# An attention layer on one core: one split of the residual, norm weights folded into the matrices, another order of its stages

## The chip, the core and the metric

One core of one Trainium2 chip runs the whole program in one launch. The metric is the device time in microseconds of that launch; the median of several runs is compared. TensorE multiplies matrices into PSUM, VectorE, ScalarE and GpSimd work elementwise, and SyncE's queue issues nearly all DMAs.

## What is computed

A two-layer decoder trunk, 512 tokens of width 1024, float32. Layer 0 is a gated linear attention and a convolutional FFN. The change lies in layer 1, a sparse attention (NSA) of 16 query heads over 4 key/value heads, followed by another FFN. Cut to what matters:

```python
kv = (rmsnorm(x, g_kv) @ w_kv)          # 6 parts: raw k, raw v, k_sel, v_sel, k_win, v_win
k_cmp, v_cmp = compress_blocks(kv[0]), compress_blocks(kv[1])   # gelu(blocks @ w1) @ w2
k_sel, k_win = rope(kv[2]), rope(kv[4])
h = rmsnorm(x, norm_mix[1])
q, gates = split(h @ w_in); gates = sigmoid(gates)
o = gates[0] * softmax(q k_cmp) v_cmp + gates[1] * softmax(rope(q) k_sel) v_sel \
  + gates[2] * softmax(rope(q) k_win) v_win
x = x + o @ w_o
```

With 512 tokens the selection takes all blocks and the window all keys, so the selected and the window branch are causal attentions with their own keys and values. `rmsnorm(x, g)` is `x * r * g` with one factor `r` per token and one weight `g` per feature.

## The kernel before

Every large product is made of three float32r products: a weight and an activation are each split into a high part `h` (ScalarE copies to float32r) and a low part `l` (the rest, by a subtraction), and `mm3` (lines 207 to 211) adds h*h, l*h and h*l. `load_w` (142) loads a matrix of 128 x 1024 into one of three `w_raw` buffers by SyncE's queue, and writes `w_h` on ScalarE and `w_l` on VectorE, or on GpSimd with `pool=True`; two buffers each. `split_x` (160) makes the eight splits of the residual `xT` times a norm weight; `squares` and `rms` (187, 200) make the token factor: the sum of squares partly on GpSimd, `rc` by a power on GpSimd, then `pb` (four transposes on TensorE) and `rb` on ScalarE.

The layer is `nsa_att` (582). Ahead of the heads it makes, each with 24 TensorE products: the first two queries `Q` (`query`, 621), the gates (607), the four key tiles (`keys_in`, 648), the raw keys and values (`raw_in`, 724, with VectorE's `kb`), and `compress` (678): VectorE's `blk`, products `ph` in two halves of 16, Gelu on ScalarE into `G`, products `pk`. `values_in` (662) makes V in 96 products of 256 columns. `rope` (593) swaps halves through one buffer `sw` by four DMAs and multiplies on GpSimd (`rot`, `sw`), and VectorE adds; `queries` (629) makes `q_s` of it.

The loop over 16 heads (892) interleaves `scores(h+1)` with `values(h)`. `scores` (769) makes for each block of 128 tokens `sc` on TensorE, the maximum `nm` on VectorE, the exponential `p_t` and its sum `su` on ScalarE, and scales `p_t`, by the engine that a letter of SCALE_ENGINE names (P is GpSimd, D VectorE, A ScalarE; places (i, b) = 00, 01, 10, 11, 20, 21, 30, 31). `values` (824) transposes `p_t` into `tp`, splits it into `pt_h` and `pt_l`, and multiplies with V into `po`; every second head closes a tile `o` with its split `o_h`, `o_l` (863). Queries and parts of the output product `pw` (`wo_part`, 579) are placed behind heads by QUERY_HEAD and WO_HEAD with a lowered priority. A scheduler sets the final order of each engine's queue from program order and priorities; each queue then runs strictly in that order.

## Time and profile before

| | |
|---|---|
| median of 3 runs | 1355.27 us (1353.68 to 1357.93) |
| the profiled execution | 1355.55 us |
| its span | 1353.8 us |
| TensorE busy | 1321.1 us (98%) |
| VectorE, ScalarE, GpSimd busy | 909.4, 617.4, 171.5 us |

The rows further down come from one profiled execution; times count from the start of its span. The layer begins where the last product of layer 0's FFN ends, at about 627.6 us, its heads run from about 757 to 955, and the rest of the output product ends at about 980. An engine's idle time ahead of an instruction stands in square brackets with what ended it.

### The profile page before, as it was taken

What the parts mean: (1) busy time and instruction counts of PE and PEld (TensorE: products, weight loads), DVE (VectorE), ACT (ScalarE), POOL (GpSimd) and SP (SyncE); (2) the same over time, 40 slices, a digit from 0 to 9 for tenths busy, and PEclk for the clock granted to TensorE, in tenths of its full rate; (3) what the DMA queues carried; (4) which work ended last, traced back from release to release, by engine and by line L of the source; (5) the groups of instructions that cost most, each with busy time, mean ns of one, the idle gap of its engine ahead of it and who ended that gap; (6) DMA issues with size and microseconds to landing.
All of it is one profiled execution on the core that took longest, in us unless ns stands there. A gap on an engine that the chain in (4) does not pass through costs nothing. (4 is left out here: it accounts for less than half of the span.)

```text
span 1353.8 us, 17497 instructions
## 1 busy us (share of the span) xinstructions
PE 1321.1 (98%) x6592; PEld 1082.1 (80%) x6592; DVE 909.4 (67%) x1408; ACT 617.4 (46%) x1032; POOL 171.5 (13%) x238
## 2 busy tenths in 40 slices
PE   8999999999999999999989999999999999999998
PEld 4988987888888888887779777777788888888886
DVE  6877665477636763674875898988767735773671
ACT  4444434344413431443436677777644423441341
POOL 3000001200000000003322444442200000000000
...
GB/s 181 75 63 63 61 50 78 94 94 94 96 95 104 95 93 93 94 82 146 127 174 63 73 46 35 44 55 32 89 114 94 93 96 98 103 93 94 94 109 63
DMA packets 40261, 119.79 MB, mean 88 GB/s; under 512 B 5344, under 2 KB 6240, under 8 KB 40176
## 3 DMA queue, kind: packets, MB, share of 16 engines
...
q14 instruction: 33, 0.27, 0.1%
...
## 5 line engine op out<-in xcount | busy, mean ns | idle before, releaser
L148 ACT ACTIVATE w_h<-w_raw 128x1024 fp32r<-128x1024 f32 (+3 forms) x198 | 200.2, 1011 | 312.9 <-PE pd L211 129.9
L211 PE MATMUL pu<-x_l,w_h 128*128 128x512 f32 x704 | 274.1, 389 | 0.0
L209 PE MATMUL pu<-x_h,w_h 128*128 128x512 f32 x704 | 274.1, 389 | 0.0
L210 PE MATMUL pu<-x_h,w_l 128*128 128x512 f32 x704 | 273.9, 389 | 0.0
L150 DVE TENSOR_TENSOR w_l<-w_raw,w_h 128x1024 fp32r<-128x1024 f32 (+3 forms) x184 | 221.1, 1202 | 50.8 <-ACT w_h L148 48.8
L211 PEld LDWEIGHTS pu<-x_l,w_h 128*128 128x128 f32 x704 | 132.2, 188 | 27.5
L210 PEld LDWEIGHTS pu<-x_h,w_l 128*128 128x128 f32 x704 | 132.2, 188 | 27.4
L209 PEld LDWEIGHTS pu<-x_h,w_h 128*128 128x128 f32 x704 | 132.2, 188 | 27.2
L209 PE MATMUL pd<-m_h,w_h 128*128 128x512 f32 x304 | 120.2, 395 | 0.0
L211 PE MATMUL pd<-m_l,w_h 128*128 128x512 f32 x304 | 120.1, 395 | 0.0
L210 PE MATMUL pd<-m_h,w_l 128*128 128x512 f32 x304 | 120.0, 395 | 0.0
L258 DVE TENSOR_TENSOR u<-pu,rb 128x512 f32<-128x512 f32 x88 | 60.6, 689 | 83.1 <-PE pu L211 81.0
L236 DVE TENSOR_TENSOR xall<-xall,pd 128x512 f32<-128x512 f32 x40 | 27.5, 688 | 100.9 <-PE pd L211 100.9
L257 POOL MEMSET u<- 128x2 f32 x88 | 8.4, 100 | 604.3 <-DVE cv L263 604.3
L155 ACT ACTIVATE m_h<-cv 128x512 fp32r<-128x512 f32 x44 | 27.8, 631 | 115.6 <-DVE cv L266 115.6
L796 ACT ACTIVATE p_t<-sc,nm 128x128 f32<-128x128 f32 (+3 forms) x128 | 66.9, 528 | 11.9 <-DVE nm L789 7.5
L260 ACT ACTIVATE cv<-u,cols 128x512 f32<-128x512 f32 x88 | 71.1, 808 | 2.6 <-DVE u L258 1.8
L209 PEld LDWEIGHTS pd<-m_h,w_h 128*128 128x128 f32 x304 | 57.1, 188 | 14.1 <-ACT m_h L155 0.4
L211 PEld LDWEIGHTS pd<-m_l,w_h 128*128 128x128 f32 x304 | 57.1, 188 | 14.0 <-DVE m_l L157 0.2
L263 DVE SCALAR_TENSOR_TENSOR cv<-u,cols,cv 128x512 f32<-128x512 f32 x88 | 66.2, 752 | 3.0
L210 PEld LDWEIGHTS pd<-m_h,w_l 128*128 128x128 f32 x304 | 57.1, 188 | 13.7
L262 DVE SCALAR_TENSOR_TENSOR cv<-u,cols,cv 128x512 f32<-128x512 f32 x88 | 65.7, 747 | 2.0 <-ACT cv L260 1.9
...
## 6 DMA issues: line engine op xcount, KB each, us to landing
w_raw<-in_ffn_up_dram SPq DMA_DIRECT2D x88, 512.0 KB, 3.6
w_raw<-in_ffn_down_dram SPq DMA_DIRECT2D x32, 512.0 KB, 3.5
w_raw<-in_gla_v_dram SPq DMA_DIRECT2D x8, 512.0 KB, 3.6
w_raw<-in_gla_r_dram SPq DMA_DIRECT2D x8, 512.0 KB, 3.6
w_raw<-in_gla_o_dram SPq DMA_DIRECT2D x8, 512.0 KB, 3.6
w_raw<-in_nsa_q_dram SPq DMA_DIRECT2D x8, 512.0 KB, 3.6
w_raw<-in_kv_f_dram SPq DMA_DIRECT2D x8, 512.0 KB, 3.7
...
```

Of the source, the lines that this page charges most:

```text
L148: ACT.activation(h, raw, AF.Copy)
L150: (POOL if pool else DVE).tensor_tensor(l, raw, h, OP.subtract)
L155: ACT.activation(h, src, AF.Copy)
L209: PE.matmul(ps, wh, xh, start=first, stop=False)
L210: PE.matmul(ps, wl, xh, start=False, stop=False)
L211: PE.matmul(ps, wh, xl, start=False, stop=last)
L236: DVE.tensor_tensor(xT[d], xT[d], ps, OP.add)
L258: DVE.tensor_tensor(u[:, 2:], ps, rb[0], OP.mult)
L260: ACT.activation(c, u[:, 2:2 + S], AF.Identity, scale=col(w, 3 * jj + 2), bias=col(f"conv_b{layer}", jj))
L262: DVE.scalar_tensor_tensor(c, u[:, 1:1 + S], col(w, 3 * jj + 1), c, OP.mult, OP.add)
L263: DVE.scalar_tensor_tensor(c, u[:, 0:S], col(w, 3 * jj), c, OP.mult, OP.add)
L796: ACT.activation(pr[i, b], scv[:, bi], AF.Exp, bias=nm[:, i, b:b + 1], accum_out=su[:, i, b:b + 1])
```

## The change

The residual is split once, without a norm weight; the norm weights `kv` and `mix1` are multiplied into the rows of each raw matrix in its buffer, on GpSimd, ahead of its split (21 matrices). Ahead of the heads come the raw keys and values first, then two of the four key tiles, the first query, `compress` with `values_in` around it, the gates and the second query; `scores(0)` comes last. Six queries and the other two key tiles go between heads (FILL). Query weights' low halves move from GpSimd to VectorE. Per head, two more of the eight scalings of `p_t` go from VectorE to GpSimd, and `o_l` goes there too. `kx` gets another buffer group.

```diff
--- before.py
+++ after.py
@@ -27,8 +27,8 @@
 ATT_END = 1664
 INTERLEAVE = "ssvsvsvsvs"
 SCORE_GROUPS = ((0, 1), (3, 2))
-SCALE_ENGINE = "PDDDDDAP"
-QUERY_HEAD = (0, 2, 4, 6, 8)
+SCALE_ENGINE = "PDDPDPAP"
+FILL = {0: ("q", (0, 1)), 1: ("q", (1, 1)), 3: ("q",), 4: ("q",), 6: ("q",), 8: ("q",)}
 WO_HEAD = (9, 10, 10, 11, 11, 12, 12, 14)
 
 COLS = {}
@@ -48,7 +48,7 @@
                ("conv_w0", 132), ("conv_w1", 132), ("conv_b0", 44), ("conv_b1", 44)])
 
 
-TAGS = {"sq0": "y1", "x_h": "xs", "x_l": "xs", "kx": "pt_h", "gz": "pt_h", "lo": "sq", "o_t": "sq", "w2": "sq", "qn": "qo", "o_h": "qo", "o_l": "qo", "kb": "qo",
+TAGS = {"sq0": "y1", "x_h": "xs", "x_l": "xs", "kx": "qo", "gz": "pt_h", "lo": "sq", "o_t": "sq", "w2": "sq", "qn": "qo", "o_h": "qo", "o_l": "qo", "kb": "qo",
         "pz": "ps", "pvt": "tp", "pqk": "ps", "plv": "ps", "pc": "pn", "pb": "pn", "pgt": "pn", "pC": "pn", "pT": "pn",
         "ph": "pj", "pk2": "pj", "G": "sq", "gr": "rot", "blk": "p_t", "w1": "pt_l", "w1b": "pt_h", "w1c": "p_t"}
 TAGS.update({f"scan{n}": "scan" for n in (64, 128, 256)})
@@ -139,10 +139,14 @@
         at = COLS[name][0] + i
         return cols[:, at:at + n]
 
-    def load_w(src, shape, raw=None, pool=False):
+    def load_w(src, shape, raw=None, pool=False, gain=None):
+
         if raw is None:
             raw = T(shape, F32, "w_raw")
             nc.sync.dma_start(raw, src)
+        if gain is not None:
+            with tc.high_priority(offset=300):
+                POOL.tensor_tensor(raw, raw, col(*gain, shape[1])[:, :, None].to_broadcast(shape), OP.mult)
         with tc.high_priority(offset=300):
             h = T(shape, F32R, "w_h")
             ACT.activation(h, raw, AF.Copy)
@@ -210,19 +214,19 @@
         PE.matmul(ps, wl, xh, start=False, stop=False)
         PE.matmul(ps, wh, xl, start=False, stop=last)
 
-    def proj(src, xs, name, w=None, pool=False, m=128):
+    def proj(src, xs, name, w=None, pool=False, m=128, gain=None):
         n = len(xs)
-        h, l = w or load_w(src, [128, n, m], pool=pool)
+        h, l = w or load_w(src, [128, n, m], pool=pool, gain=gain and (gain, 0))
         ps = P(name)
         for k in range(n):
             mm3(ps[0:m], (h[:, k], l[:, k]), xs[k], k == 0, k == n - 1)
         return ps
 
-    def proj_tok(src, xs, name):
+    def proj_tok(src, xs, name, gain=None):
 
         pv = [P(name) for _ in range(2)]
         for kp in range(2):
-            h, l = load_w(src[kp], [128, 4, 256])
+            h, l = load_w(src[kp], [128, 4, 256], gain=gain and (gain, 4 * kp))
             for kk in range(4):
                 k = 4 * kp + kk
                 for i in range(4):
@@ -580,11 +584,10 @@
         add_x(d, proj(a["nsa_o"][d][:, k0:k0 + 4], os_[k0:k0 + 4], "pw", pool=k0 == 0))
 
     def nsa_att():
-        xq = [split_x("mix1")]
+        xs = [split(xT[k], "x") for k in range(KT)]
         acc = squares()
-        early = [proj(a["nsa_q"][0], xq[0], "tp")]
+        first = proj(a["kv_f"][0], xs, "sc", gain="kv")
         rb, r4 = rms(acc)
-        early.append(proj(a["nsa_q"][1], xq[0], "tp"))
         cosT = T([128, S], F32, "cosT")
         sinT = T([128, S], F32, "sinT")
         nc.sync.dma_start(cosT, a["rope"][0])
@@ -605,7 +608,7 @@
         gate = T([128, 4, 3, 16], F32, "gate")
 
         def gates():
-            pg = proj(a["nsa_g"], xq[0], "po", m=48)
+            pg = proj(a["nsa_g"], xs, "po", m=48, gain="mix1")
             gz = T([48, S], F32, "gz")
             DVE.tensor_tensor(gz, pg[0:48], rb[0:48], OP.mult)
             pgt = P("pgt")
@@ -619,7 +622,7 @@
         Q = []
 
         def query():
-            ps = early[len(Q)] if len(Q) < 2 else proj(a["nsa_q"][len(Q)], xq[0], "pl", pool=True)
+            ps = proj(a["nsa_q"][len(Q)], xs, "pl", gain="mix1")
             q = T([128, S], F32, "qn")
             DVE.scalar_tensor_tensor(q, ps, 0.125, rb, OP.mult, OP.mult)
             Q.append(q)
@@ -645,22 +648,21 @@
 
 
         K = [T([128, 2, S], F32R, f"K{g}") for g in range(4)]
-        def keys_in(br):
-            for ft in range(2):
-                ps = proj(a["kv_f"][4 + 2 * br + ft], xk[0], "sc")
-                k = T([128, S], F32, "kx")
-                DVE.tensor_tensor(k, ps, rb, OP.mult)
-                kr = rope(k)
-                for hh in range(2):
-                    hs = slice(hh * 64, hh * 64 + 64)
-                    kt = K[2 * ft + hh]
-                    ACT.activation(kt[0:64, br], kr[hs], AF.Copy)
-                    DVE.tensor_tensor(kt[64:128, br], kr[hs], kt[0:64, br], OP.subtract)
+        def keys_in(br, ft, name="sc"):
+            ps = proj(a["kv_f"][4 + 2 * br + ft], xs, name, gain="kv")
+            k = T([128, S], F32, "kx")
+            DVE.tensor_tensor(k, ps, rb, OP.mult)
+            kr = rope(k)
+            for hh in range(2):
+                hs = slice(hh * 64, hh * 64 + 64)
+                kt = K[2 * ft + hh]
+                ACT.activation(kt[0:64, br], kr[hs], AF.Copy)
+                DVE.tensor_tensor(kt[64:128, br], kr[hs], kt[0:64, br], OP.subtract)
 
         V = [T([128, 4, 4, 128], F32R, f"V{br}") for br in range(2)]
 
         def values_in(br):
-            pv = proj_tok(a["kv_v"][br], xk[0], "pvt")
+            pv = proj_tok(a["kv_v"][br], xs, "pvt", gain="kv")
             for i in range(4):
                 src = pv[i // 2][:, (i % 2) * 256:(i % 2) * 256 + 256].rearrange("p (h d) -> p h d", h=4)
                 ACT.activation(V[br][:, i, :, 0:64], src, AF.Copy, scale=r4[:, i:i + 1])
@@ -722,7 +724,7 @@
                 DVE.tensor_tensor(Vc[:, :, 64:128], pkv, Vc[:, :, 0:64], OP.subtract)
 
         def raw_in(f):
-            ps = proj(a["kv_f"][f], xk[0], "sc")
+            ps = proj(a["kv_f"][f], xs, "sc", gain="kv") if f else first
             kb = T([128, 2, 256], F32, "kb")
             for hh in range(2):
                 for par in range(2):
@@ -860,7 +862,7 @@
             ACT.activation(lo[hs], o_ps[64:128], AF.Copy)
             DVE.tensor_tensor(half[0][hs], o_ps[0:64], lo[hs], OP.add)
             if gi % 2:
-                os_.append(split(half[0], "o"))
+                os_.append(split(half[0], "o", POOL))
             yield
 
         def run(g, n=99):
@@ -868,26 +870,21 @@
                 if next(g, 1):
                     return
 
+        for f in range(4):
+            raw_in(f)
+        keys_in(0, 0)
+        keys_in(1, 0)
         query()
-        xk = [split_x("kv")]
         queries(0)
+        compress("k")
+        values_in(1)
+        compress("v")
         gates()
-        keys_in(0)
+        values_in(0)
         query()
-        raw_in(0)
-        keys_in(1)
-        raw_in(1)
-        raw_in(2)
-        raw_in(3)
-        compress("k")
-        compress("v")
         run(scores(0))
         queries(1)
-        values_in(1)
-        values_in(0)
-        xq[0] = split_x("mix1")
         compressed(0)
-        query()
         compressed_t(0)
         for h in range(16):
             gs = scores(h + 1) if h + 1 < 16 else None
@@ -906,9 +903,12 @@
                 compressed_t(h // 4 + 1)
             if h % 2 == 1 and h // 2 + 2 < 8:
                 queries(h // 2 + 2)
-            if h in QUERY_HEAD:
+            for f in FILL.get(h, ()):
                 with tc.high_priority(offset=-50):
-                    query()
+                    if f == "q":
+                        query()
+                    else:
+                        keys_in(*f, name="pl")
             for d in range(KT):
                 if WO_HEAD[d] == h:
                     with tc.high_priority(offset=-50):
```

GpSimd's queue where the layer begins, before (`sq` sums the squares, `rc` is the norm factor, `rot` and `sw` are the rope's products):

```order
L196 TENSOR_TENSOR sq<-sq 128x512 x5
L706 MEMSET BD 128x256
L686 MEMSET G 128x256 x2
L184 TENSOR_TENSOR rc<-ms,mhalf 128x4
L600 TENSOR_TENSOR rot<-qn,cosT 128x512
L601 TENSOR_TENSOR sw<-sw,sinT 128x512
L640 TENSOR_TENSOR q_s<-rot,q_s 64x512 x2
```

and now:

```order
L200 TENSOR_TENSOR sq<-sq 128x512 x3
L149 TENSOR_TENSOR w_raw<-w_raw,cols 128x1024
L200 TENSOR_TENSOR sq<-sq 128x512
L149 TENSOR_TENSOR w_raw<-w_raw,cols 128x1024
L200 TENSOR_TENSOR sq<-sq 128x512
L149 TENSOR_TENSOR w_raw<-w_raw,cols 128x1024
L708 MEMSET BD 128x256
L688 MEMSET G 128x256
L149 TENSOR_TENSOR w_raw<-w_raw,cols 128x1024 x2
L188 TENSOR_TENSOR rc<-ms,mhalf 128x4
L688 MEMSET G 128x256
L149 TENSOR_TENSOR w_raw<-w_raw,cols 128x1024 x4
```

The scaling of five weights has moved in front of `rc`, four more stand right behind it.

ScalarE's queue around `compress`, before (`K` are copies of a key tile, `G` is Gelu, `p_t` the exponentials of head 0):

```order
L657 ACTIVATE K_5066<-rot 64x512
L148 ACTIVATE w_h<-w_raw 128x1024
L657 ACTIVATE K_5067<-rot 64x512
L148 ACTIVATE w_h<-w_raw 128x1024
L696 ACT_TABLE_LOAD
L696 ACTIVATE G<-ph 128x4x31
L796 ACT_TABLE_LOAD
L796 ACTIVATE p_t,su<-sc,nm 128x128 x2
L696 ACT_TABLE_LOAD
L696 ACTIVATE G<-ph 128x4x31
L796 ACT_TABLE_LOAD
L796 ACTIVATE p_t,su<-sc,nm 128x256 x2
```

and now:

```order
L659 ACTIVATE K_5034<-rot 64x512
L659 ACTIVATE K_5035<-rot 64x512
L152 ACTIVATE w_h<-w_raw 128x1024
L659 ACTIVATE K_5034<-rot 64x512
L659 ACTIVATE K_5035<-rot 64x512
L698 ACT_TABLE_LOAD
L698 ACTIVATE G<-ph 128x4x31 x2
L641 ACTIVATE q_s<-rot 64x512 x2
L152 ACTIVATE w_h<-w_raw 128x384
L668 ACTIVATE V_5039<-pvt,rc 128x4x64
L152 ACTIVATE w_h<-w_raw 128x1024
```

Gelu's table is loaded once, behind the copies of both key tiles; the exponentials are no longer between.

GpSimd's queue at the same place now (`kx` are the two key tiles, `qn` the first query):

```order
L149 TENSOR_TENSOR w_raw<-w_raw,cols 128x1024 x4
L603 TENSOR_TENSOR rot<-kx,cosT 128x512
L604 TENSOR_TENSOR sw<-sw,sinT 128x512
L603 TENSOR_TENSOR rot<-kx,cosT 128x512
L149 TENSOR_TENSOR w_raw<-w_raw,cols 128x384
L603 TENSOR_TENSOR rot<-qn,cosT 128x512
L604 TENSOR_TENSOR sw<-sw,sinT 128x512
L149 TENSOR_TENSOR w_raw<-w_raw,cols 128x1024 x2
L604 TENSOR_TENSOR sw<-sw,sinT 128x512
```

The query's `rot` stands ahead of the second key tile's `sw`; before, `rot` and `sw` of the first query stood ahead of all four key tiles, as the fence on the layer's beginning shows.

GpSimd's queue from there to the first head, before:

```order
L600 TENSOR_TENSOR rot<-kx,cosT 128x512 x2
L601 TENSOR_TENSOR sw<-sw,sinT 128x512 x3
L814 TENSOR_TENSOR p_t<-p_t,su 128x128
L814 TENSOR_TENSOR p_t<-p_t,su 128x512
L600 TENSOR_TENSOR rot<-qn,cosT 128x512
L640 TENSOR_TENSOR q_s<-rot,q_s 64x512 x2
L752 TENSOR_TENSOR pcm<-pcm,mx 128x512
```

and now:

```order
L603 TENSOR_TENSOR rot<-qn,cosT 128x512
L816 TENSOR_TENSOR p_t<-p_t,su 128x128
L816 TENSOR_TENSOR p_t<-p_t,su 128x256
L604 TENSOR_TENSOR sw<-sw,sinT 128x512
L149 TENSOR_TENSOR w_raw<-w_raw,cols 128x1024
L643 TENSOR_TENSOR q_s<-rot,q_s 64x512
L816 TENSOR_TENSOR p_t<-p_t,su 128x512
L816 TENSOR_TENSOR p_t<-p_t,su 128x384
L643 TENSOR_TENSOR q_s<-rot,q_s 64x512
L754 TENSOR_TENSOR pcm<-pcm,mx 128x512
L816 TENSOR_TENSOR p_t<-p_t,su 128x128
```

Ahead of the scalings (3,1) and (2,1) of head 0 (512 and 384 columns) there are now a weight and a `q_s`; before, head 0 had one scaling of 128 and one of 512 columns there.

## Rows read from the trace of the kernel before

**Rows 1.** The page's first part, whole execution: busy us (share of the span) and instructions of each engine; PEld is TensorE's weight load.

```profile
PE 1321.1 (98%) x6592; PEld 1082.1 (80%) x6592; DVE 909.4 (67%) x1408; ACT 617.4 (46%) x1032; POOL 171.5 (13%) x238
```

**Rows 2.** Busy times by stretch, of the first part of the layer and of its heads. Columns: stretch, its length, busy us and instructions of TensorE, its weight loads, VectorE, ScalarE and GpSimd, then the granted TensorE clock (1.00 is full speed), the DMA engines' share and GB/s.

```profile
627.60:757.00 129.40, 120.32 (x704) 101.92 (x704) 89.88 (x150) 62.64 (x102) 37.72 (x27) 0.97 0.43 128
757.00:955.00 198.00, 193.15 (x1125) 147.36 (x1125) 176.46 (x359) 146.82 (x376) 78.29 (x70) 1.00 0.17 43
```

**Rows 3.** Timeline of TensorE in the layer: the instructions ahead of which it stood idle, eight of them in order of time. Columns: start us, length us, engine, line, operation, output<-inputs, shapes, count, and the idle time with what ended it.

```profile
635.43 0.32 PE L175 MATMUL pb<-kc,rc 128*128 128x128 f32 x1 [1.03 <-POOL rc L184]
...
648.80 0.26 PE L613 MATMUL pgt<-kc,gz 48*128 48x48 f32 x1 [0.55 <-DVE gz L610]
...
676.53 0.50 PE L210 MATMUL sc<-x_h,w_l 128*128 128x512 f32 x1 [0.90 <-DVE w_l L150]
...
701.67 0.76 PE L785 MATMUL sc<-K,q_s 128*128 128x512 f32 x1 [4.24 <-DVE kb L729]
...
750.41 0.49 PE L211 MATMUL pl<-x_l,w_h 128*128 128x512 f32 x1 [0.55 <-DVE x_l L167]
...
752.55 0.50 PE L209 MATMUL pl<-x_h,w_h 128*128 128x512 f32 x1 [1.64 <-ACT x_h L165]
...
823.40 0.30 PE L842 MATMUL tp<-kc,p_t 128*128 128x128 f32 x1 [1.53 <-DVE pt_l L846]
...
875.16 0.30 PE L842 MATMUL tp<-kc,p_t 128*128 128x128 f32 x1 [1.54 <-DVE pt_l L846]
```

**Rows 4.** Busy times by stretch, of the 5.33 us behind the 4.24 us of idleness; columns as in rows 2.

```profile
701.67:707.00 5.33, 5.33 (x23) 4.81 (x24) 3.89 (x11) 1.28 (x1) 0.00 (x0) 0.50 0.63 216
```

**Rows 5.** Timeline of TensorE in layer 0's FFN: two products of a projection that follow each other.

```profile
560.74 0.39 PE L211 MATMUL pu<-x_l,w_h 128*128 128x512 f32 x1
560.97 0.39 PE L209 MATMUL pu<-x_h,w_h 128*128 128x512 f32 x1
```

**Rows 6.** Timeline of VectorE and of GpSimd around 820 us, ahead of the wait at 823.40: three scalings on VectorE, one scaling and two `q_s` on GpSimd.

```profile
819.71 2.94 DVE L816 TENSOR_SCALAR p_t<-p_t,su 128x128 f32<-128x128 f32 x3
...
819.50 0.40 POOL L814 TENSOR_TENSOR p_t<-p_t,su 128x128 f32<-128x128 f32 x1 [3.81 <-DVE su L806]
...
819.86 2.64 POOL L640 TENSOR_TENSOR q_s<-rot,q_s 64x512 fp32r<-64x512 f32 x2
```

**Rows 7.** Groups of VectorE's instructions from 580 to 960 us, shapes apart. Columns: line, engine, operation, output<-inputs, shapes, count | busy us, mean ns of one | idle us ahead of them and what ended it.

```profile
L816 DVE TENSOR_SCALAR p_t<-p_t,su 128x384 f32<-128x384 f32 x32 | 22.5, 738 | 0.4
...
L789 DVE TENSOR_REDUCE nm<-sc 128x1 f32<-128x512 f32 x32 | 21.6, 679 | 5.8 <-PE sc L787 5.7
...
L150 DVE TENSOR_TENSOR w_l<-w_raw,w_h 128x1024 fp32r<-128x1024 f32 x15 | 21.4, 1426 | 4.7 <-ACT w_h L148 4.6
...
L816 DVE TENSOR_SCALAR p_t<-p_t,su 128x256 f32<-128x256 f32 x32 | 19.0, 633 | 0.0
...
L683 DVE TENSOR_TENSOR blk<-kb,cols 128x124 f32<-128x124 f32 x32 | 11.6, 434 | 0.1
...
L729 DVE TENSOR_TENSOR kb<-sc,rb 64x256 f32<-64x256 f32 x16 | 6.7, 422 | 0.4
...
L816 DVE TENSOR_SCALAR p_t<-p_t,su 128x128 f32<-128x128 f32 x16 | 4.9, 308 | 0.2
```

**Rows 8.** Groups of GpSimd's instructions, whole execution, shapes apart; columns as in rows 7.

```profile
L814 POOL TENSOR_TENSOR p_t<-p_t,su 128x512 f32<-128x512 f32 x16 | 17.9, 1120 | 46.4 <-DVE su L806 32.8 <-ACT p_t L796 11.0 <-ACT q_s L638 2.4
...
L150 POOL TENSOR_TENSOR w_l<-w_raw,w_h 128x1024 fp32r<-128x1024 f32 x6 | 14.4, 2401 | 5.1 <-ACT w_h L148 5.1
...
L814 POOL TENSOR_TENSOR p_t<-p_t,su 128x128 f32<-128x128 f32 x16 | 6.5, 406 | 64.7 <-DVE su L806 52.8 <-PE sc L785 7.4 <-ACT p_t L796 4.5
```

**Rows 9.** Timeline of SyncE's queue (the load that takes the second weight's buffer) and of GpSimd (`rc`) at the start of the layer.

```profile
630.01 0.33 SPq L145 DMA_DIRECT2D w_raw<-in_kv_f_dram  x1
...
634.15 1.22 POOL L184 TENSOR_TENSOR rc<-ms,mhalf 128x4 f32<-128x4 f32 x1
```

**Rows 10.** The page's part on DMA issues: output<-input, queue, count, KB of one, median us from issue to landing.

```profile
w_raw<-in_kv_f_dram SPq DMA_DIRECT2D x8, 512.0 KB, 3.7
```

**Rows 11.** Timeline of GpSimd: the rope product that waits for the first query's `sw` (that query, `qn`, was done at 637.44).

```profile
641.48 1.30 POOL L601 TENSOR_TENSOR sw<-sw,sinT 128x512 f32<-128x512 f32 x1 [2.67 <-DMA sw<-qn]
```

**Rows 12.** Timeline of ScalarE: two copies of a key tile, a load of Gelu's table, and Gelu.

```profile
664.17 1.29 ACT L657 ACTIVATE K<-rot 64x512 fp32r<-64x512 f32 x2 [3.99 <-DVE rot L602]
...
696.57 1.28 ACT L696 ACT_TABLE_LOAD   x1 [2.16 <-PE ph L694]
...
697.86 0.27 ACT L696 ACTIVATE G<-ph 128x124 f32<-128x124 f32 x1
```

**Rows 13.** The chain of work that ended last, in order of time: start us, length us, what; a half of `compress`, and the compressed scores of one group of heads.

```profile
712.34 3.71 PE ph L694 x32
...
731.14 1.73 PE pC L745 x16
```

**Rows 14.** Busy times by stretch, of the instructions on the score tiles `sc` alone, in the heads; TensorE's 269 are three to a score.

```profile
757.00:955.00 198.00, 64.45 (x269) 29.96 (x183) 52.78 (x90) 69.35 (x233) 1.00 0.17 43
```

**Rows 15.** Timeline of GpSimd, VectorE and TensorE at the end of the heads: the last 512-column scaling, the last `o_l`, and the product that reads it.

```profile
949.59 1.18 POOL L814 TENSOR_TENSOR p_t<-p_t,su 128x512 f32<-128x512 f32 x1 [5.91 <-DVE su L806]
...
959.05 0.69 DVE L157 TENSOR_TENSOR o_l<-o_t,o_h 128x512 fp32r<-128x512 f32 x1
...
959.79 0.50 PE L211 MATMUL pw<-o_l,w_h 128*128 128x512 f32 x1
```

## The prediction

> **What bounds the kernel now.** First the page's busy shares: TensorE is busy for 1321.1 of 1353.8 us [rows 1]. The change touches one stage and leaves the number of TensorE's large products alone, so it can only win or lose time in which TensorE stands still or runs slowly there. Next the busy times by stretch [rows 2]: in the first part of the layer (627.6 to 757, ahead of the heads) TensorE is busy for 120.3 of 129.4 us, in the sixteen heads (757 to 955) for 193.15 of 198.0. In the heads VectorE is busy for 176.5 of the 198 us, GpSimd for 78.3 (40%): TensorE leads, VectorE is close behind. Then TensorE's timeline with the idle time ahead of each instruction and what ended it [rows 3]: 4.24 us before the first score product (it waits for VectorE's `kb`, since TensorE's queue is in order), 1.64 and 0.55 us for the second `mix1` splits, 0.90 for a weight's low half, 0.55 for the gates, 1.03 for the norm factor `rc`, and in the heads twice 1.5 us. Last the granted clock: right after the 4.24 us of idleness TensorE ran 5.33 us at 0.50 [rows 4], the lower of its two levels, which cost about half of that, 2.67 us. The rate of a projection is 0.227 us a product [rows 5], 24 of them 5.44 us.
>
> The sum is made against the profiled execution, 1355.55 us (span 1353.8 and 1.75 around it), 0.28 above the median of 1355.27. A measurement of this kernel can tell some 0.3% (4.1 us) from no change.
>
> **What it removes.** (1) Scores of head 0 no longer stand ahead of `compress` and `values_in`; the 4.24 us wait and the slow 5.33 us behind it have lost their cause: 4.24 + 2.67 = 6.9. (2) The second `mix1` split is gone (one plain split serves all projections): 0.55 + 1.64 = 2.2. (3) The gates' transposes now have 8 products of `values_in(0)` ahead of them, about 1 us, which covers 0.55. (4) The 0.90 us at 676.53 came while VectorE did `kb`, `blk` and weights at once; the place is gone, what comes instead is (b). Together 10.6 us. (5) In the heads, the 1.5 us waits have a visible cause [rows 6]: three `p_t` scalings on VectorE took 2.94 us because GpSimd was in `q_s`; three by their means [rows 7] are 1.6. VectorE keeps three of five scalings per head and loses the eight `o_l` subtractions, so less of it can be blocked. I count these two waits, 1.53 + 1.54 = 3.1; ends: 0 and all idle time of the heads, 198.0 - 193.15 = 4.85.
>
> **What it adds.** Each of 21 weights now passes GpSimd before its split. The trace has no such multiplication. Nearest rows: `p_t` times a broadcast column, 1.12 us for 512 columns, so 2.24 for 1024, and a subtraction of two 1024-column tiles, 2.40 [rows 8]. I take 2.24, the operand being broadcast in both. With three `w_raw` buffers, a weight has some 8 us between landing and need, so most are hidden by the projections in between. Where they are not:
>
> (a) `rc`. In GpSimd's queue `rc` now stands behind the scaling of the fifth weight. The load in that place of SyncE's queue was issued at 630.01 [rows 9] and takes 3.7 us [rows 10], so it lands at 633.7; its scaling ends at about 635.9, where `rc` started at 634.15. Behind `rc` wait TensorE's `pb` transposes, ScalarE's `rb`, then every `kb`: 1.03 becomes about 2.6, so 1.6 more. Ends 0 (a quicker landing) and 2.4.
>
> (b) VectorE behind the first six projections. Per raw projection: 4 `kb` of 0.422, 8 `blk` of 0.434, one `w_l` of 1.426 [rows 7] make 6.6 us against 5.44 on TensorE. Four of them, from `rb` on (about 10.7 us into the layer), end at some 37.6, while the seventh weight is wanted at about 37.0: 0.6. Ends 0 and 2.
>
> (c) `compress`. GpSimd multiplies `rot` of the first query before `sw` of the second key tile, and ScalarE loads Gelu's table only behind the copies of that key tile. The chain: the query's product ends 5.44 us after its start; its `qn` on VectorE stands behind the rotation of the first key tile, whose `sw` needs about 4 us of DMA after the key (as `sw` of the query did, which GpSimd took up at 641.48 [rows 11]), and comes at about 8.1. Then `rot` and `sw` on GpSimd, 1.3 each, the sum on VectorE 0.7 (a 512-column subtraction of [rows 15] takes 0.69), two `K` copies 1.29, the table 1.28, Gelu 0.27 [rows 12], and 0.3 for hand-overs: about 14.5. TensorE has used 5.44 + 1 for `values_in`, then waits for `qn` (1.2), does the first half of `compress` (3.71 [rows 13]) and 15 products of 0.12, and stands at 13.6 for the buffer that Gelu frees: 0.9. With 0.4 for the late `w_l` ahead of it: 2.5. Ends 0 and 6.
>
> (d) Start of the heads. Nothing hides the first scores' latency but a projection. Up to the second group of transposes TensorE has 11.0 us of work: nine scores, 5.0 (90 keep it busy for 64.45 [rows 14], 0.72 each, of which the modelled end overlaps the next by 0.16, as a product of 0.39 does at a rate of 0.227 [rows 5]), the compressed scores 1.73 [rows 13], 17 projection products 3.9, four transposes 0.4. VectorE, from the last query's end on, needs about 9.8 us to the second `su`: one `w_l` 1.43, two `p_t` 0.9, maxima and other 512-column passes of up to 0.68 [rows 7], and short ones. Then GpSimd ends `q_s` (to about 11.3) and scales 512 columns (1.12) and 384 (0.88, between the 128 and 512 column rows): 13.3. So 2.3. Ends 0 and 4.3 (the two scalings blocked as in [rows 6]).
>
> (e) End of the heads. `o_l` of the last pair goes to GpSimd, 1.3 instead of 0.69, and the third product on `o_l` started 0.05 after it [rows 15]: 0.6. The last 384-column `p_t` stands behind the 512-column one on GpSimd: 949.59 + 1.18 + 0.88 = 951.65, where TensorE went on at 951.04: 0.6. Together 1.2; ends 0 and 1.5.
>
> Edits at nothing: one split instead of three frees VectorE and ScalarE off the path; eight projections between heads instead of five are the same TensorE work elsewhere; seven table loads fewer lie on ScalarE, which is last in only one wait of [rows 3], counted in (2). On SyncE's queue the loads of `compress` move ahead among the weights, some 0.4 us of issue each, and the key tiles' `sw` loads move behind them; with weights landing 8 us ahead of need this is covered, and if that cover is gone, the price is that of (c).
>
> Sum: -10.6 - 3.1 + 1.6 + 0.6 + 2.5 + 2.3 + 1.2 = -5.5; 1355.55 - 5.5 = 1350.0 us.
>
> **A rule weighed.** The trace first: the 128-column `p_t` on VectorE has a mean of 308 ns, the 256-column one 633 and the 384-column one 738 [rows 7], and a run of three took 2.94 us during GpSimd's work [rows 6]. The Trainium skill ("SBUF — State Buffer", section "Who interferes with whom") states that VectorE's fast two-port modes, and its instructions with two SBUF inputs against a GpSimd instruction that reads SBUF, share one port pair with GpSimd, and whichever comes second is blocked for the whole instruction. The trace agrees with it, in that one scaling waits out a whole `q_s`. By this rule the change's own GpSimd work takes back what VectorE is freed of, and term (5) is 0 or turns against the change; that is the third rival.
>
> **The rivals.**
>
> *Larger gain.* The chains (c) and (d) come out at their lower ends, as GpSimd and the DMAs are a little earlier than I put them, and all idle time of the heads goes: -10.6 - 4.85 + 1.6 + 0.6 + 1.2 = -12; 1343.5 us. For it: VectorE had 176.5 of 198 us and sheds about 22 + 6. Against: TensorE's queue is in order, so each late tile counts. Chance 0.2.
>
> *The stalls only move.* The new waits in (a), (c), (d) bring the lower clock again: two more stretches like the one of [rows 4] cost 2 x 2.67: 1350.0 + 5.3 = 1355.3. For it: 4.24 us of idleness preceded that stretch and my new waits are 1 to 2.6 us each; against: TensorE stood for 1.64 us at 752.55 [rows 3], and the heads' stretch behind it has a mean granted clock of 1.00 [rows 2]. Chance 0.15.
>
> *Slower: GpSimd sets the pace of the heads.* Its load there rises from 78 us by 16 x (0.64 + 0.88) for the new scalings, 10 for `o_l`, some 9 for four weights and 5 for two key tiles, less 12 for the query splits that go [rows 8]: about 114 of 198 us (58%). Its queue is in order: a `p_t` behind a `sw` that waits for a DMA, or behind a weight, holds the transposes. It decides where the second scaling, 0.88, is what the transposes wait for; in the eight heads with projections that is 8 x 0.9 = 7, and the 3.1 of (5) is lost: 1350.0 + 7 + 3.1 = 1360.1 us. For it: at a load of 40% it already blocks VectorE in [rows 6]. Against: no TensorE wait of [rows 3] ends on GpSimd's `p_t`, and with eight projections the early heads are longer for TensorE. Chance 0.2.
>
> **How the numbers follow.** Forecast 0.45, its own range 1347 to 1354 by the ends of (b) to (e); two thirds of it lie below 1351.2. Faster by over 0.3% (below 1351.2): 0.31 + 0.2 = 0.51. Within (to 1359.3): 0.14 + 0.15 + 0.03 of the slower rival = 0.32. Slower: 0.17. The range takes in the first rival to 1342 and the third to 1361.
>
> **What would show it.** Right: no idle time over 3 us before a score product, no stretch at half clock in the middle of the layer, `pb` waiting about 2.6 us for `rc`, a wait of about 1 us before the second half of `compress`, one of 2 us before the transposes of head 0, no 1.5 us waits in the heads. Wrong: TensorE waiting on GpSimd's `p_t` or `w_raw` in many heads (third rival), new stretches at 0.50 (second), or a layer from 627.6 to 955 shorter by over 9 us (first).

## The result and the profile after

The changed kernel takes 1371.61 us (median of 4 runs), 1.0118 times the kernel before (95% interval 1.0103 to 1.0134): some 16 us slower, outside the range of 1342 to 1361 and on the other side of the forecast. The profiled execution took 1369.42 us, its span 1367.6.

The profile's first part, columns as in [rows 1]:

```profile
PE 1326.8 (97%) x6592; PEld 1085.3 (79%) x6592; DVE 905.1 (66%) x1358; ACT 597.9 (44%) x1009; POOL 233.1 (17%) x293
```

GpSimd has 61.6 us more than in [rows 1], VectorE only 4 less. Busy times by stretch, columns as in [rows 2]: the first two lines are the part ahead of the heads with head 0, and the other heads; then the four stretches in which the clock fell.

```profile
624.70:756.00 131.30, 118.11 (x701) 98.86 (x699) 89.12 (x136) 43.62 (x85) 57.08 (x41) 0.97 0.38 116
756.00:969.00 213.00, 204.18 (x1132) 155.52 (x1130) 170.76 (x325) 147.10 (x370) 113.86 (x110) 0.97 0.17 45
636.08:639.49 3.41, 3.41 (x11) 2.75 (x10) 2.01 (x5) 0.60 (x1) 0.85 (x1) 0.50 0.85 303
673.63:677.04 3.41, 3.20 (x15) 3.20 (x16) 1.28 (x2) 0.00 (x0) 3.11 (x2) 0.50 0.47 153
796.51:803.33 6.82, 6.82 (x25) 4.48 (x24) 4.53 (x9) 5.27 (x15) 4.04 (x5) 0.50 0.04 11
960.35:967.17 6.82, 6.82 (x23) 5.59 (x23) 3.04 (x5) 2.78 (x5) 1.28 (x1) 0.50 0.00 0
```

TensorE's timeline, all waits in the layer of over 1 us, as in [rows 3]:

```profile
635.82 0.90 PE L179 MATMUL pb<-kc,rc 128*128 128x128 f32 x4 [3.23 <-POOL rc L188]
671.68 0.39 PE L215 MATMUL pvt<-w_l,x_h 128*128 128x256 f32 x1 [1.11 <-DVE w_l L154]
673.84 1.00 PE L696 MATMUL ph<-blk,w 128*128 128x124 f32 x3 [1.18 <-DVE qn L627]
682.62 0.60 PE L696 MATMUL ph<-blk,w 128*128 128x124 f32 x3 [1.65 <-ACT G L698]
701.01 0.71 PE L696 MATMUL ph<-blk,w 128*128 128x124 f32 x4 [1.05 <-ACT G L698]
743.15 0.44 PE L844 MATMUL tp<-kc,p_t 128*128 128x128 f32 x2 [2.02 <-DVE p_t L818]
747.46 0.50 PE L836 MATMUL po<-pt_h,V 128*128 128x512 f32 x1 [1.20 <-ACT pt_h L846]
796.16 0.39 PE L836 MATMUL po<-pt_l,V 128*128 128x256 f32 x1 [2.14 <-DVE pt_l L848]
959.61 0.44 PE L844 MATMUL sc<-kc,p_t 128*128 128x128 f32 x2 [1.02 <-POOL p_t L816]
```

The 4.24 us among the first scores are gone and so are the waits for the second split. In their place stand nine others of 1 to 3.2 us. Four of them (3.23, 1.18, 2.14, 1.02) have one of the slow stretches at their end or within 0.8 us behind it; the 2.02 us at 743 and the 1.65 at 682 have none.

The table counts TensorE in the layer, from the last product of layer 0's FFN to the first of layer 1's: its length in the profiled execution, TensorE's idle time in it (sum over the timeline), and the time at 0.50 (half of it is lost). Length less idle time less that half is 331 to 338 us in every kernel, so the two columns carry most of the difference. They come from one execution each, whose time can lie some 4 us off the median (e2's took 1361.4, e4's 1369.1). Ratios are to the kernel before, run beside each.

| kernel | median us | ratio (95% interval) | layer | idle | at 0.50 |
|---|---|---|---|---|---|
| before | 1354.3 to 1356.5 | 1 | 351.6 | 14.0 | 6.8 |
| changed | 1371.6 | 1.0118 (1.0103 to 1.0134) | 367.5 | 22.0 | 20.5 |
| e1 changed, scalings of before | 1368.3 | 1.0092 (1.0077 to 1.0107) | 365.1 | 21.8 | 17.1 |
| e2 before, new scalings | 1357.8 | 1.0022 (1.0011 to 1.0033) | 356.1 | 13.1 | 17.1 |
| e3 changed, no gains | 1356.3 | 1.0010 (1.0000 to 1.0021) | 356.1 | 15.0 | 13.7 |
| e14 e3 and e1 together | 1353.7 | 0.9985 (0.9976 to 0.9994) | 348.9 | 12.5 | 3.4 |
| e11 before, gains of one | 1374.5 | 1.0148 (1.0134 to 1.0162) | 371.8 | 28.1 | 20.5 |
| e13 gains nobody waits for | 1376.2 | 1.0160 (1.0141 to 1.0179) | 373.0 | 25.6 | 23.9 |
| e5 gains on ScalarE | 1363.6 | 1.0065 (1.0048 to 1.0081) | 358.9 | 15.7 | 17.1 |
| e4 changed, `pb` later | 1373.2 | 1.0124 (1.0105 to 1.0143) | 367.2 | 20.8 | 23.9 |
| e12 changed, wait filled | 1371.6 | 1.0127 (1.0112 to 1.0142) | 365.9 | 19.5 | 17.1 |
| e6 changed, keys ahead | 1372.1 | 1.0125 (1.0107 to 1.0142) | 370.7 | 22.5 | 23.9 |
| e10 changed, scores covered | 1370.7 | 1.0120 (1.0105 to 1.0135) | 368.7 | 20.4 | 34.1 |
| e7 before, values ahead | 1350.4 | 0.9971 (0.9961 to 0.9982) | 346.3 | 11.3 | 0 |
| e8 before, new scalings but the last | 1356.6 | 1.0015 (1.0003 to 1.0026) | 352.6 | 12.0 | 10.2 |
| e9 e7 and scalings in heads 1 to 14 | 1349.5 | 0.9958 (0.9946 to 0.9970) | 345.4 | 9.7 | 0 |

The granted clock over the span is known for every execution, not only the profiled one. One minus it, times the span, is the time that the lower level cost, to within 0.7 us. On the mean of the executions that is about 6 us before and 14.7 changed; 10.9 in e1, 9.2 in e2, 6.9 in e3, 5.4 in e14. Without that time the kernel before takes 1349, the changed kernel 1357, e1 1357, e2 1349, e3 1350 and e14 1348. So of the 16 us some 9 are the clock and some 8 standing still.

### The profile page after: what moved, and what is told of

Same layout as the page of the kernel before. It is cut to its first block, busy times and chain, and to the rows that moved or that the text cites. A ratio compares the mean times of both kernels' runs of the same rounds, so it can differ in the third digit from the quotient of the medians.

```text
span 1367.6 us, 17488 instructions
## 1 busy us (share of the span) xinstructions
PE 1326.8 (97%) x6592; PEld 1085.3 (79%) x6592; DVE 905.1 (66%) x1358; ACT 597.9 (44%) x1009; POOL 233.1 (17%) x293
## 3 DMA queue, kind: packets, MB, share of 16 engines
q10 hardware_dynamic: 576, 1.05, 0.2%
## 4 chain that ended last, share of the span: by engine, by line
PE 82%; DVE 9%; ACT 3%; POOL 2%; issue 2%; DMA 1%; SPq 0%; DVEq 0%; POOLq 0%; ACTq 0%
PE pu L215 12%; PE pu L214 12%; PE pu L213 12%; PE pd L213 6%; PE pd L215 6%; PE pd L214 6%; PE pw L213 2%; PE pw L214 2%; PE pw L215 2%; PE po L836 2%; PE plv L477 2%; PE tp L844 2%; DVE w_l L154 2%; PE pv L213 1%; PE pv L214 1%
## 5 line engine op out<-in xcount | busy, mean ns | idle before, releaser
L154 DVE TENSOR_TENSOR w_l<-w_raw,w_h 128x1024 fp32r<-128x1024 f32 (+3 forms) x190 | 234.9, 1236 | 56.7 <-ACT w_h L152 54.5
L798 ACT ACTIVATE p_t<-sc,nm 128x128 f32<-128x128 f32 (+3 forms) x128 | 66.8, 529 | 21.5 <-DVE nm L791 20.8
L214 PEld LDWEIGHTS pd<-m_h,w_l 128*128 128x128 f32 x304 | 57.1, 188 | 13.7
```

The costliest lines, as they stand in the source:

```text
L154: (POOL if pool else DVE).tensor_tensor(l, raw, h, OP.subtract)
L214: PE.matmul(ps, wl, xh, start=False, stop=False)
L798: ACT.activation(pr[i, b], scv[:, bi], AF.Exp, bias=nm[:, i, b:b + 1], accum_out=su[:, i, b:b + 1])
```

## The experiments

The diffs are cut to the lines that matter.

### The change in three parts

**e1** (changed kernel) and **e2** (kernel before) move the scalings alone:

```diff
-SCALE_ENGINE = "PDDPDPAP"          # e1; e2 has it the other way round
+SCALE_ENGINE = "PDDDDDAP"
-                os_.append(split(half[0], "o", POOL))
+                os_.append(split(half[0], "o"))
```

> The changed kernel with the five-to-one part of the head scalings undone: SCALE_ENGINE as before and o_l on VectorE again; everything else of the change stays. In the changed kernel the layer is 15.9 us longer than before (367.9 against 352.0), of it about 7.7 in more idle time of TensorE and 7.5 in four stretches at half clock in place of one. Theory A (GpSimd's new load in the heads, that is p_t and o_l, makes the stalls of the heads and the two stretches at half clock that begin at 796.5 and 960.4): TensorE's idle time in the heads falls from about 13.4 to near 7 and both stretches go (3.4 us each): 10 us less, about 1360. Theory B (the heads' stalls come from the weights, queries and key tiles that were moved into heads 0 to 2): the stalls at 743 to 796 stay, the one at 959.6 alone goes: 1 to 4 us less, about 1367 to 1370.

> The kernel before with that part alone: SCALE_ENGINE as in the change, and o_l on GpSimd. Theory A: the heads lose what the first experiment gives back, about 5 to 10 us: 1361 to 1366. Theory B: little, since the kernel before has no weights or key tiles on GpSimd in its heads: 1355 +- 2. A gain of 3 (the prediction's fifth term) would give 1352.

Both came out at about 3 us: e1 gave back 1371.6 - 1368.3, e2 lost 0.22%. That is theory B for e1; e2 lies between the theories, nearer to B. By the clocks above the whole of it is the clock: 14.7 against 10.9 us, and 9.2 against about 6, with as much time left without it. In e1 the stretch behind the end of the heads is gone and the stalls of heads 0 to 2 stay. In e2 TensorE's timeline shows what the part does:

```profile
755.27 0.50 PE L209 MATMUL pl<-x_h,w_h 128*128 128x512 f32 x1 [2.80 <-ACT x_h L165]
953.29 0.44 PE L842 MATMUL sc<-kc,p_t 128*128 128x128 f32 x2 [1.02 <-POOL p_t L814]
```

The two waits of 1.5 us [rows 3] don't occur any more, so idle time falls from 14.0 to 13.1. But ahead of the third query TensorE waits 2.80 us in place of 0.55 and 1.64 [rows 3], 0.6 more; the last transposes wait 1.02 us; and behind each of these the clock is at half for 3.41 us (756.93 to 760.35 and 954.91 to 958.32, mean 0.50). A third new stretch of 3.41 us stands behind the 1.03 us ahead of `pb`, which the edit left as they were.

**e3** leaves the 21 multiplications out.

```diff
-        if gain is not None:
+        if False:
```

> The changed kernel without the 21 multiplications of weights on GpSimd (the two norm weights are then left out of the result). Theory A: the wait for rc falls from 3.23 to about 1.4 and the half-clock stretch behind it goes (1.8 + 1.7), the weight's low half at 671.7 is in time (1.1), the stretch at 673.6 may go (1.7), in the heads little: 4 to 6 us less, about 1365 to 1367. Theory B (weights on GpSimd also hold up the heads, through VectorE's blocked instructions at 796): also the 2.1 at 796 and the stretch behind it, 3.4: 10 to 12 less, about 1360.

15 us came back, more than either theory had; by the clocks above some 8 of them are the clock (14.7 against 6.9). Its timeline:

```profile
633.74 0.65 PE L179 MATMUL pb<-kc,rc 128*128 128x128 f32 x4 [0.78 <-POOL rc L188]
674.65 1.16 PE L696 MATMUL ph<-blk,w 128*128 128x124 f32 x8 [1.63 <-ACT G L698]
785.92 0.58 PE L836 MATMUL po<-pt_l,V 128*128 128x256 f32 x1 [2.46 <-DVE pt_l L848]
```

Ahead of the first scores idle time is 2.4 us in place of 8.3, no stretch at half clock is left there, and the first scores start 94.1 us into the layer in place of 104.2. The stall of head 2 stays, so that one isn't the gains' (theory B had it so); it belongs to the order, with its fill between heads.

**e14** is e3 with the edit of e1: the order, the single split and the fill alone (with the query weights' low halves on VectorE and the other buffers of `kx`, which no run separates).

> The changed kernel without the multiplications of weights (the two norm weights are left out of the result) and with the scalings of before, so that the order of the stages, the single split and the fill between heads are what is left of the change. Theory A (the parts add up; the scalings cost about 3 in either kernel): 1356.3 - 3 = 1353.3, that is, the 10 us that the prediction took off ahead of the heads are spent again at their start and in heads 0 to 2. Rival (without GpSimd's load the new order gives what the prediction's first four terms say): 1345 to 1349.

1353.7, theory A. Taken one after the other, the order gives -0.15% (about -2 us), the scalings +3 and the gains +15. That these make +16 follows from the steps. What is measured is that the scalings cost about the same (2.6 to 3.5 us) with the old order (e2) and with the new, with the gains (e1) or without (e3 against e14). Gains and order don't add up so: see e11.

### Why the gains cost 15 us

**e11** does the gains alone in the kernel before (a column of ones in place of the norm weights).

```diff
+            if ones and shape != [128, 4, 128]: POOL.tensor_tensor(raw, raw, ones[0][:, 0:shape[1], None].to_broadcast(shape), OP.mult)
             h = T(shape, F32R, "w_h")
```

> The kernel before with that part alone: GpSimd multiplies each weight of the layer's projections, but those of the output, by a column of ones in its buffer ahead of the split (the result keeps its values). Theory A (a weight on GpSimd costs VectorE about 1.7 us whichever order the projections have, and more where TensorE waits for a low half): 8 to 15 us more, 1362 to 1369. Rival (it is the changed order, raw projections first, that leaves no slack for it): 1355 to 1359.

+20 us, above theory A. The rival is out: the old order has no slack for them either. VectorE's `kb`, late by 4.24 us before, is now late by 1.92 and 6.58, and the clock is at half for 10.24 us around it. So the split by parts depends on which comes first: with the gains already there, order, single split and fill take 6 to 8 us off (e1 against e11), without them 2.

**e5** puts the same multiplications on ScalarE.

```diff
-                POOL.tensor_tensor(raw, raw, col(*gain, shape[1])[:, :, None].to_broadcast(shape), OP.mult)
+                for k in range(shape[1]): ACT.activation(raw[:, k], raw[:, k], AF.Copy, scale=col(gain[0], gain[1] + k))
```

> The changed kernel with the weights' gains multiplied in the same buffers by ScalarE, in eighths (quarters for the value weights), in place of GpSimd; each weight is ready as late or later, ScalarE gets about 2 us per weight, VectorE and GpSimd nothing. Without any gain the changed kernel took 1356.3. Theory A (it is GpSimd's reading and writing of a whole weight that holds up VectorE: at 623.9 and 627.9 additions of 0.68 us take 2.4): nearly all of the 15 us come back: 1357 to 1361. Rival (the weights are split too late, whichever engine multiplies): 1366 to 1371.

1363.6, between the two: about half comes back. Ahead of the first scores idle time is 5.75 us, between e3's 2.4 and 8.3; the longest waits there are 2.24 us for `G` at 683.05, and 1.13 and 1.24 ahead of `pc` and `pb`, behind the squares that ScalarE makes among its multiplications.

**e13** keeps GpSimd as busy and lets no weight wait for it.

```diff
-                POOL.tensor_tensor(raw, raw, col(*gain, shape[1])[:, :, None].to_broadcast(shape), OP.mult)
+                for k in range(2 if shape[2] > 48 else 1): POOL.tensor_tensor(spare[0], spare[0], raw[:, k, 0:1].to_broadcast([128, S]), OP.add)
```

> The changed kernel in which GpSimd, in place of each weight's multiplication, adds one of the weight's columns to the cosine table in two operations of 128x512: about as long on GpSimd and with the same reads of SBUF, but no split of a weight waits for it (the norm weights are left out of the result, and the rope's table is changed). Without any of that work the changed kernel took 1356.3, with the multiplications 1371.6. Theory A (GpSimd's working in SBUF holds up VectorE and its own queue): 1366 to 1372. Rival (the weights are split 2 us later, and TensorE's queue waits for them): 1356 to 1360.

1376.2, above theory A; two additions take 2.4 us, a multiplication 2.1. The rival is out: no product on a `w_h` or `w_l` in the layer has any idle time ahead of it. (Loads do come later: SyncE's queue waits eleven times, 29.5 us in all, for a buffer that an addition reads; TensorE doesn't wait for a weight for it.) A weight that is split late isn't needed to lose the time; GpSimd's work is enough. Where GpSimd multiplies, two things happen. First, in the changed kernel, VectorE stands still inside its instructions. VectorE's timeline and GpSimd's at the layer's start:

```profile
618.69 2.38 DVE L161 TENSOR_TENSOR x_l<-xall,x_h 128x512 fp32r<-128x512 f32 x1
621.00 0.67 DVE L240 TENSOR_TENSOR xall<-xall,pd 128x512 f32<-128x512 f32 x1
623.28 0.68 DVE L161 TENSOR_TENSOR x_l<-xall,x_h 128x512 fp32r<-128x512 f32 x1
627.93 2.38 DVE L161 TENSOR_TENSOR x_l<-xall,x_h 128x512 fp32r<-128x512 f32 x1
632.06 0.16 DVE L186 TENSOR_SCALAR ms<-pc 128x4 f32<-128x4 f32 x1 [1.15 <-PE pc L207]
632.14 2.75 DVE L154 TENSOR_TENSOR w_l<-w_raw,w_h 128x1024 fp32r<-128x1024 f32 x1
...
617.98 2.55 POOL L149 TENSOR_TENSOR w_raw<-w_raw,cols 128x1024 f32<-128x1024 f32 x1
620.49 1.74 POOL L200 TENSOR_TENSOR sq<-sq 128x512 f32<-128x512 f32 x1
...
627.16 2.60 POOL L149 TENSOR_TENSOR w_raw<-w_raw,cols 128x1024 f32<-128x1024 f32 x1 [0.52 <-DMA w_raw<-in_kv_f_dram]
631.91 1.90 POOL L149 TENSOR_TENSOR w_raw<-w_raw,cols 128x1024 f32<-128x1024 f32 x1 [2.14 <-DMA w_raw<-in_kv_f_dram]
633.76 2.00 POOL L188 TENSOR_TENSOR rc<-ms,mhalf 128x4 f32<-128x4 f32 x1
```

The same subtraction takes 0.68 us alone and 2.38 beside a multiplication; the addition at 621.00, with one input in PSUM, runs at its usual 0.67 beside GpSimd's `sq`. The Trainium skill ("SBUF — State Buffer", section "Who interferes with whom") has such blocking for VectorE instructions with two SBUF inputs; these rows agree. `ms` was ready at 632.2, but GpSimd had taken up the fifth weight at 631.91, so `rc` came 1.5 us later and took 2.00 in place of 1.22 [rows 9]. Further on the same two causes add up. The first key tile on VectorE, behind the four raw projections, in the changed kernel and in e3:

```profile
637.39 1.75 DVE L731 TENSOR_TENSOR kb<-sc,rb 64x256 f32<-64x256 f32 x4 [2.50 <-ACT rb L181]
662.02 0.69 DVE L654 TENSOR_TENSOR kx<-sc,rb 128x512 f32<-128x512 f32 x1
...
635.05 1.75 DVE L731 TENSOR_TENSOR kb<-sc,rb 64x256 f32<-64x256 f32 x4 [1.06 <-ACT rb L181]
656.09 0.69 DVE L654 TENSOR_TENSOR kx<-sc,rb 128x512 f32<-128x512 f32 x1
```

Counted from the start of the layer (625.12 and 626.14) it comes 7.0 us later, at 36.9 in place of 29.9. The first `kb` is 3.4 us late already, behind `rc`; nearly all the rest are three entries of VectorE's timeline (two of eight `blk`, one `w_l`) that are 1.1 to 1.2 us longer beside multiplications.

Second, GpSimd's queue is in order, and what stands behind a weight is late too. In e13 this can be followed through four engines, in head 2, where no weight's split is involved (GpSimd, VectorE, TensorE):

```profile
779.04 4.52 POOL L150 TENSOR_TENSOR cosT<-cosT,w_raw 128x512 f32<-128x512 f32 x4
783.52 0.97 POOL L815 TENSOR_TENSOR p_t<-p_t,su 128x128 f32<-128x128 f32 x2
784.45 1.26 POOL L603 TENSOR_TENSOR sw<-sw,sinT 128x512 f32<-128x512 f32 x1
...
785.75 0.69 DVE L604 TENSOR_TENSOR rot<-rot,sw 128x512 f32<-128x512 f32 x1 [4.72 <-POOL sw L603]
787.13 1.40 DVE L659 TENSOR_TENSOR K<-rot,K 64x512 fp32r<-64x512 f32 x2 [0.23 <-ACT K L658]
788.57 0.69 DVE L626 SCALAR_TENSOR_TENSOR qn<-pl,rb 128x512 f32<-128x512 f32 x1
...
789.31 0.90 PE L746 MATMUL pC<-BD,qn 128*128 128x64 f32 x3 [4.46 <-DVE qn L626]
```

Four additions hold `sw` for 4.5 us, VectorE's queue waits 4.72 us in order for it, `qn` stands behind, and TensorE waits 4.46. That wait is e13's own; the changed kernel's stall in head 2 stays without the gains (e3). From the layer's start to the first scores VectorE is busy for 56.4 us in e13, 64.9 in the changed kernel and 51.4 in e3. So VectorE was lengthened less than half as much in e13, and the first scores still come at 102.3 us of the layer, against 104.2 and 94.1. How the 15 us of the change divide between the two ways isn't settled.

### Single waits and the clock

**e4** writes the second raw projection between `rc` and `pb`.

```diff
-        r4 = rsqrt_cols(pc)
+        r4 = rsqrt_cols(pc); mid and mid()       # mid makes the second raw projection
```

> The changed kernel with the second raw projection written between rc and pb, so that pb stands 20 products (4.5 us) later in TensorE's queue; GpSimd's order is the same. Theory A (the wait for rc and the half clock behind it are a loss of their own): the idle 3.23 us and half of the 3.41 us stretch go, 4.9 us less: about 1366.5. Rival (VectorE, which gets the first kb later, is what the raw projections wait for in either case): the wait comes back before the fourth raw projection or before ph, 0 to 2 us less: about 1370.

The rival in kind, without its gain (1373.2 for 1370) and two projections later: the 3.23 us go, and TensorE waits 0.84 and 3.42 us for the first `w_l` of the fifth and sixth projections, with 6.83 us at half clock around the second. In VectorE's queue that `w_l` stands behind `kb` and 15 `blk`, which had to wait for `rb` in either kernel: the wait of the prediction's term (b). But the edit itself makes `rb` 1.9 us and the first `kb` 3.9 us later in the layer than in the changed kernel, so how much of it (a) hides there isn't shown.

**e12** fills the same wait with products.

```diff
+        for _ in range(0 if fill is None else 15): PE.matmul(pc[:, 128:512], fill[:, 0:128], fill[:, 0:384], start=True, stop=True)
```

> The changed kernel with 15 products of 384 columns, whose result nobody reads, on TensorE between pc and pb, so that most of the 3.23 us wait for rc is busy (15 x 0.17 = 2.6 us) and not shorter. Theory A (TensorE's standing still there is what brings the lower clock): the 3.41 us at half clock from 636.1 are gone, 1.7 less, about 1370; the idle time ahead of pb is about 0.6. Rival (the stretch comes from something else at that place): it stays, and the time is 1371.6 or a little more.

TensorE around that place, and the granted clock of the 5.2 and 3.43 us there:

```profile
635.26 2.77 PE L209 MATMUL pc<-x_h 128*128 128x384 f32 x15
638.67 0.65 PE L179 MATMUL pb<-kc,rc 128*128 128x128 f32 x4 [0.40 <-POOL rc L188]
...
635.50:640.70 5.20, 4.80 (x27) 4.17 (x26) 2.93 (x3) 0.60 (x1) 3.38 (x3) 1.00 0.87 278
639.07:642.50 3.43, 3.43 (x18) 2.84 (x17) 2.42 (x5) 0.60 (x1) 0.98 (x1) 1.00 0.81 295
```

The stretch at half clock is gone, with `pb` as late in the layer as before (10.7 us) and TensorE busy ahead of it: theory A for the place. The other profiles agree: the seven kernels whose `pb` waits 1.24 us or more (changed, e1, e5, e6, e10, e11, e13) have a stretch around that wait or within 1.4 us behind it, and e4, where it doesn't wait, has none there. The time didn't fall (1371.6): a later wait, for Gelu, was 3.15 us in place of 1.65, with 6.83 us at half clock around its end. So the clock's part is shown at one place and not as a gain.

**e8** has the new scalings in heads 0 to 14 alone.

```diff
+SCALE_ENGINE = "PDDPDPAP"
+                        eng = (SCALE_ENGINE if h < 15 else "PDDDDDAP")[2 * i + b]
+                os_.append(split(half[0], "o", POOL if h < 15 else DVE))
```

> The kernel before with the changed scalings and o_l on GpSimd in heads 0 to 14 alone; head 15 as before. With all heads it took 1357.8, with the two 1.5 us waits gone from the heads, but 1.02 us of new idle time at the last transposes, a stretch of 3.41 us at half clock right behind it (1.7), and 1.2 us more ahead of the split for the third query. Theory A: the new idle time at the end and the half clock behind it go together, 2.7 less: about 1355. Rival (the slow stretch belongs to the end of the heads and not to that wait): 1 less, 1356.8.

In the profile heads 4 to 15 lose 1.0 of idle time and 1.7 to the clock less than in e2, as theory A has it: no wait and no slow stretch at their end. The medians show 0.07%, about 1 us, within their intervals: 1356.6 is the rival's time, not theory A's 1355, so the 1.7 us of the clock aren't shown as a gain.

**e6** and **e10** move the fill and the first scores of the changed kernel.

```diff
-        values_in(0)
-        query()
         run(scores(0))        # e6: the key tiles of FILL ahead of query(), the rest as it is
+        values_in(0)
+        query()               # e10
```

> The changed kernel with the two key tiles of heads 0 and 1 (FILL) made ahead of the heads, behind values_in(0). Theory A (the stall of head 2, 0.99 + 2.14 us ahead of po at 793 to 796, and the 6.83 us at half clock behind it come from rot, sw and w_raw of the fill standing in GpSimd's queue and blocking VectorE there): 3 + 3.4 less, about 1365. Rival (TensorE needs the fill between heads 0 and 2 since VectorE and GpSimd set the pace there): the stalls come elsewhere in heads 0 to 3, within 2 us of 1371.

> The changed kernel with the first scores ahead of values_in(0) and the second query, so that 16 us of products lie between the first scores and the transposes of head 0. Theory A (the 4.9 us of idle time from the first scores to the end of head 0 are the scores' latency with nothing beside it): that falls to 1 to 2 us, 3 to 4 less, about 1368. Rival (GpSimd and VectorE are late there anyway, with w_raw, sw and q_s in their queues): the idle time stays or moves into the first scores' bank waits, within 1.5 of 1371.6.

Both rivals: the stalls move. In e6 heads 1 to 3 have 2.6 us of idle time in place of 4.8, but the start of the heads waits 2.50 us for `p_t` and 2.53 for `pcm`, each time on GpSimd; in e10 `pcm` is waited for 3.84 us at 750.07, again on GpSimd, and head 2 for 1.83 and 2.42.

### A version that beats both

**e7** moves one line of the kernel before; **e9** adds the new scalings in heads 1 to 14, with e8's line for `o_l`.

```diff
         raw_in(3)
+        values_in(1)
         compress("k")
...
-        values_in(1)
         values_in(0)
```

> The kernel before with one line moved: values_in(1) ahead of compress, so that 10.9 us of products stand between the raw projections and the first scores, and VectorE has the time to make kb and blk. Theory A (the prediction's first term is a real loss that only this order gives back): 4.24 idle and 3.4 at half clock go, 1347 to 1348. Rival (the start of the heads then has only values_in(0) as cover, as in the changed kernel): waits of 3 to 5 us and a stretch at half clock come there, 1352 to 1356.

> The kernel before with values_in(1) ahead of compress (1350.4 by itself) and, in heads 1 to 14, the changed scalings; o_l on GpSimd except in the last pair. Theory A (the gains are of separate places): the two waits of 1.53 us that are left in the heads go, and no new one comes at their end: 1350.4 - 3 = 1347.4. Rival (GpSimd's load at the start of the heads holds up the second split or the first transposes there, as the 2.80 us ahead of the third query did with the scalings in all heads): 1350 to 1353.

e7 is 0.29% faster than before (0.18 to 0.39), e9 0.42% (0.30 to 0.54). The 4.24 us and the half clock behind them are gone, without the gains; the forecast of 1347 to 1348 for e7 is missed by 2.4, in part by new waits for `w_l` (0.86 and 1.14). In e9's profiled execution, one of its two fastest, the layer keeps the full clock:

```profile
625.60:971.00 345.40, 335.74 (x1933) 266.44 (x1933) 267.28 (x498) 225.06 (x501) 150.45 (x140) 1.00 0.28 80
```

Over the spans of e9's six executions the granted clock is 0.996 to 0.999, so not all of them keep it. The two 1.5 us waits went, as theory A had it, but 1.0 of the 3 us shows in the medians, 1.8 by the ratios, and the intervals of e7 and e9 overlap: that e9 beats e7 isn't shown.

## Why the prediction was wrong

The sum, -5.5, splits by the three parts, and each can be held against its own runs (in the order of e14, e3 and the changed kernel):

| part | terms | predicted | measured |
|---|---|---|---|
| order, single split, fill | (1) to (4), (c) without `w_l`, (d) | -6.2 | about -2 (e14); -6 to -8 with the gains there (e1 against e11) |
| scalings and `o_l` | (5), (e) | -1.9 | +3 (e1, e2) |
| gains | (a), (b), 0.4 of (c) | +2.6 | +15 (e3); +20 in the old order (e11) |

**The gains are the step that failed.** The prediction took 2.24 us for each multiplication (1.9 to 2.9 measured, most 1.9: about right), then said that most were hidden, since a weight lands some 8 us ahead of need. That counts TensorE's need of that weight. Of what else stands behind a multiplication in GpSimd's queue it counts `rc` alone, in (a), and of the VectorE instructions beside it none. e13 shows that the loss needs no TensorE wait for a weight. (a) was put at a wait of 2.6 and is 3.23. (b) took 6.6 us of VectorE for a raw projection; in e3 four take 21.0, some 5.3 each, about as long as TensorE, and in the changed kernel they are late by `rc` and by blocking. (Its own 10.7 + 4 x 6.6 give 37.1, not 37.6.) (c), 2.5, is 1.11 + 1.18 + 1.65 + 1.05 = 5.0; the wait for `qn` has the size forecast (1.2), but e3 has none, so it belongs to the gains; of the waits for `G` 1.63 stay in e3. Sharing with GpSimd had been weighed for the scalings in the heads and left out for the weights.

**The clock was put at nothing.** The sum took 2.67 us off with the old slow stretch and added none for the new waits; that stood as a rival of 0.15 with two stretches. There were four, 20.5 us at 0.50 against 6.8, so some 7 us in the profiled execution, and some 9 of the 16 on the mean of all.

**The removed terms were right, and were spent again.** (1) to (3) are gone from the timeline (the 4.24 us stood ahead of the third score tile, not the first; that changes nothing in the sum); for (4) another `w_l` is late by 1.11. (d), 2.3, measures 4.9 of idle time in the changed kernel, 3.2 in e3 and 2.4 in e14, without the gains and the new scalings. What the sum hadn't at all are heads 1 to 3: 0.4 us of idle time before, 4.8 after, 5.4 in e3, 3.2 in e14. The fill puts `rot`, `sw` and key copies among their scalings, and e6 shows that moving its key tiles only moves the waits.

**The scalings.** (5) was right in mechanism: both waits of 1.5 us go in e2. (e), 1.2, was right for the scaling (0.6 forecast, 0.7 measured: 1.02 in place of 0.33) and put another 0.6 on `o_l`, behind which TensorE doesn't wait at all; the clock behind it, 1.7 in e2, wasn't counted. The longer wait for the third query's split in e2 (0.6, and 1.7 of clock) had no term.

**The rivals.** That of the lower clock came true with four stretches in place of two. The slower one (GpSimd sets the pace of the heads) is nearest in time, 1360.1, but not in kind: of the waits in the heads over 0.4 us only 0.43 and 1.02 end on GpSimd's `p_t`, not many heads, and in heads 4 to 15 idle time didn't rise (4.4 before, 4.0 after). The range took the rivals one at a time, and had no case for GpSimd's work ahead of the heads.
